# Making the state's part of an SSD output transposed, with a loaded decay row and ScalarE arguments, in a hybrid SSD and attention layer

## The chip, the cores and the metric

The kernel runs on one core of one Trainium2 chip. A core has five engines with an instruction queue each: TensorE (PE; its weight loads are listed apart as PEld), VectorE (DVE), ScalarE (ACT), GpSimd (POOL) and SyncE (SP). The metric is the time of one execution on the device in microseconds (us), the median of several runs. A profiled execution gives the span and the trace.

## What is computed

One decoder layer over 512 tokens and 16 meta tokens in front of them, with model width 1024: a Mamba-2 state space (SSD) branch of 32 heads of 64 columns in 4 groups, a forgetting-attention branch, a gated sum of both, an output projection and a norm. All is float32. The change lies in the SSD branch, whose core in the reference is (cut):

```python
xdt = xh * dt                                  # per chunk of 128 tokens, per head
a_cs = jnp.cumsum(dt * a, axis=-1)             # cumulative log decay
seg = a_cs[..., :, None] - a_cs[..., None, :]
decay = jnp.exp(jnp.where(causal, seg, -jnp.inf))
cb = jnp.einsum("bclgn,bcsgn->bcgls", cm, bm)
y_diag = jnp.einsum("bcgls,bcgrls,bcsgrp->bclgrp", cb, decay, xdt)
states = jnp.einsum("bclgn,bcgrl,bclgrp->bcgrpn", bm, jnp.exp(a_cs[..., -1:] - a_cs), xdt)
# scan over chunks: h_in[c+1] = h_in[c] * exp(a_cs[c, -1]) + states[c]
y_off = jnp.einsum("bclgn,bcgrpn,bcgrl->bclgrp", cm, h_in, jnp.exp(a_cs))
y = y_diag + y_off + d_skip * x
```

The reference is `y_off`: the state h (128 state rows by 8 heads of 64 columns for a group) multiplied by C, each token's row scaled by exp of that head's cumulative decay at that token.

## The kernel before

**Matrix products.** Large products (`gemm`, L106) split both operands into a high and a low part and issue three matmuls for each slice: high by high, low by high, high by low. A weight block arrives in `raw` by a DMA of SyncE; ScalarE makes the high part `whi` (a 128x1024 cast, L90) and VectorE the low part `wlo` (L91). Their results go to one of two PSUM tiles `mm`. All other products go to one of four PSUM tiles `ax`.

**The SSD branch.** It is done group by group, `ssd_gemm(g)` and then `ssd_core(g)`. `ssd_gemm` makes x, B and C of the group (`conv`: the PSUM tile is copied by ScalarE to `xp`, L380, then four taps) and the gate z. `ssd_core` goes over five chunks: c = 0 is the 16 meta tokens, c = 1 to 4 are 128 tokens each. Channels lie on partitions (two heads of 64 in a tile of 128) and tokens along the row in x, z and the result `yd`; h has the state dimension on partitions and the group's 512 columns along the row. For each chunk:

- PE transposes x into `px` (four 128x128, L440). VectorE makes `xdt` (L443) and `xdd` (L446) of it.
- `ab`, a 128x1024 tile from the ring `big4` of four buffers, is filled by a GpSimd DMA (L449, 512 KB, each row of the cumulative decay sent to all 128 partitions). VectorE subtracts the decay of the row's own token and takes the minimum with 0, one head at a time (eight instructions, L451), ScalarE takes exp (L453), VectorE multiplies by the causal C·B product.
- `py` is C times h: the chunk of C is the stationary operand and h, 512 columns, moves (L456). ScalarE copies it to `y`, eight instructions of 64 columns, each with the decay factor `eac` of a head as scale (L460).
- `pst` is the chunk's state (L466). For the next h, GpSimd multiplies h by the chunk decay (L471) and VectorE adds `pst` (L472).
- `pt` collects the result, tokens along the row: four transposes of `y` (L477) and on top of them eight products of `xdt` with `ab`, y_diag (L481). VectorE adds it to `yd` (four instructions, L486).

An `ax` tile of a chunk takes the slot of the tile of the same kind one chunk earlier: `py` of chunk c can start only when `py` of chunk c-1 has been read.

**Around it.** While the chunks of group g run, PE fills the time between their steps with other products: in group 0 the `conv` products of the next group; in the others `s_group(g-1)`, the projection of the group that was finished before. Its 128x512 results are copied by ScalarE in `s_group(0)`, which lies among the chunks of group 1 (`ms`, L691), and added by VectorE in the others (L693). The four buffers of `big4` are shared by the groups, so the DMA of `ab` for chunk c of group g+1 waits on GpSimd's queue until y_diag of chunk c of group g has been made.

**What sets the order.** The code is written group by group, but the order of the instructions on each engine comes from a scheduler of the tile framework, which places them by its own cost model before the kernel is built; sections marked `raised` come first when ready. On the chip each engine runs its list in this fixed order: an instruction that waits holds all behind it on that engine.

## Time and profile before

| what | value |
|---|---|
| median of 3 runs | 852.7 us (852.65 to 852.73) |
| the profiled execution, its own time | 853.14 us |
| its span | 851.4 us |
| PE busy | 834.7 us, 98% |
| DVE busy | 601.8 us, 71% |
| ACT busy | 442.5 us, 52% |
| POOL busy | 72.1 us, 8% |

The span is the time between the first and the last instruction that the trace shows; the profiled execution's time is 1.74 us longer. Busy time is the union of the instructions' own durations on an engine; an engine that waits for data or for a free buffer is idle. The chunks of the four groups lie between about 90 and 405 us.

### The profile page before, as it was taken

How to read it: one execution, taken by the hardware profiler on the slowest of the kernel's cores; microseconds unless marked ns; L12 is line 12 of the kernel's file. 1: busy time of each engine (PE TensorE's matmuls, PEld its weight loads, DVE VectorE, ACT ScalarE, POOL GpSimd, SP SyncE). 2: the span in 40 equal slices, each digit the busy share in tenths (PEclk: the TensorE clock that was granted, in tenths of full speed). 3: DMA queues.
4: the chain of work that ended last, by engine and by line, in shares of the span. 5: the costliest groups of instructions: out<-in, count | busy, mean ns of one | idle time of the engine just before them, and what ended most of it. 6: DMA issues, size and time to landing. Idle time of an engine off the chain costs nothing.

```text
span 851.4 us, 13318 instructions
## 1 busy us (share of the span) xinstructions
PE 834.7 (98%) x5037; PEld 722.9 (85%) x5037; DVE 601.8 (71%) x1296; ACT 442.5 (52%) x906; POOL 72.1 (8%) x136
## 2 busy tenths in 40 slices
PE   6999999999999999999999999999999999999996
PEld 4998889778987799778898988888888898888885
DVE  7799598946994689746786766666767666647735
ACT  6455455445543366333574666566666666522332
POOL 3031110011000100011100001000000100000000
PEclk9999999999999999999999999999999999999999
DMA  7245344235332453222322222222322222224422
GB/s 214 76 127 162 78 110 112 77 96 115 89 96 79 96 123 99 88 62 51 86 91 76 75 75 76 75 76 75 77 75 76 76 75 75 75 84 166 146 75 99
DMA packets 114500, 79.94 MB, mean 94 GB/s; under 512 B 5684, under 2 KB 108260, under 8 KB 114436
## 3 DMA queue, kind: packets, MB, share of 16 engines
q1 hardware_dynamic: 110692, 70.08, 28.9%
q0 software_dynamic: 3744, 9.01, 5.2%
q8 instruction: 39, 0.64, 0.3%
q14 instruction: 25, 0.20, 0.1%
HBM read 76.65 MB, written 2.44 MB: 93 GB/s over the span
## 4 chain that ended last, share of the span: by engine, by line
PE 90%; DMA 3%; DVE 3%; issue 2%; ACT 0%; POOL 0%; SPq 0%; DVEq 0%; POOLq 0%
PE mm L106 71%; PE ax L657 3%; PE mm L781 3%; PE ax L631 2%; DMA big<-acs_d 2%; PE ax L781 1%; PE ax L481 1%; PE ax L596 1%; PE ax L466 1%; PE ax L595 1%; PE ax L456 1%; PE ax L440 1%; DMA big<-in_x_dram 1%; DVE big L451 1%; PE ax L477 1%
## 5 line engine op out<-in xcount | busy, mean ns | idle before, releaser
L106 PE MATMUL mm<-ulo,whi 128*128 128x264 f32 (+1 forms) x1024 | 286.5, 328 | 0.0
L106 PE MATMUL mm<-uhi,whi 128*128 128x264 f32 (+1 forms) x1024 | 284.5, 327 | 0.0
L90 ACT CAST whi<-raw 128x1024 fp32r<-128x1024 f32 x118 | 124.2, 1052 | 143.4 <-PE mm L106 115.4
L91 DVE TENSOR_TENSOR wlo<-raw,whi 128x1024 fp32r<-128x1024 f32 x117 | 142.8, 1220 | 68.4 <-ACT whi L90 31.5
L106 PE MATMUL mm<-uhi,wlo 128*128 128x264 f32 (+1 forms) x1024 | 189.4, 326 | 0.0
L106 PEld LDWEIGHTS mm<-uhi,whi 128*128 128x128 f32 x1024 | 172.3, 188 | 16.9 <-issue 2.7
L106 PEld LDWEIGHTS mm<-ulo,whi 128*128 128x128 f32 x1024 | 172.4, 188 | 16.3 <-issue 2.9
L106 PEld LDWEIGHTS mm<-uhi,wlo 128*128 128x128 f32 x1024 | 152.6, 188 | 14.5 <-issue 0.7
L106 PE MATMUL mm<-yhi,whi 128*128 128x512 f32 x192 | 78.6, 409 | 0.7 <-ACT ms L691 0.7
L106 PE MATMUL mm<-ylo,whi 128*128 128x512 f32 x192 | 76.6, 399 | 0.0
L601 ACT ACTIVATE tmp<-tmp,nmx 128x400 f32<-128x400 f32 (+4 forms) x80 | 41.2, 517 | 28.1 <-DVE nmx L598 26.0
L384 DVE SCALAR_TENSOR_TENSOR xbc<-xp,hcol,xbc 128x528 f32<-128x528 f32 x72 | 54.1, 763 | 0.5 <-ACT tmp L387 0.3
L106 PE MATMUL mm<-yhi,wlo 128*128 128x512 f32 x192 | 54.1, 401 | 0.0
L598 DVE CUSTOM_DVE_ANT_0 tmp<-ax,maskf 128x288 f32<-128x288 f32 (+4 forms) x80 | 32.7, 434 | 23.3 <-PE ax L596 23.0
L451 DVE TENSOR_SCALAR big<-big,dtok 128x128 f32<-128x128 f32 x128 | 28.8, 289 | 27.2 <-DMA big<-acs_d 27.2
L460 ACT ACTIVATE tmp<-ax,eac 128x64 f32<-128x64 f32 x128 | 28.2, 330 | 34.8 <-PE ax L456 34.8
L106 PEld LDWEIGHTS mm<-yhi,whi 128*128 128x128 f32 x192 | 36.1, 188 | 10.7 <-issue 2.3
L106 PEld LDWEIGHTS mm<-ylo,whi 128*128 128x128 f32 x192 | 36.1, 188 | 9.5 <-issue 2.6
L106 PEld LDWEIGHTS mm<-yhi,wlo 128*128 128x128 f32 x192 | 35.8, 188 | 9.2 <-issue 2.2
L657 PE MATMUL ax<-big,vt 128*128 128x512 f32 (+2 forms) x144 | 35.4, 329 | 0.0
L453 ACT ACTIVATE big<-big 128x1024 f32<-128x1024 f32 x16 | 17.0, 1061 | 33.9 <-DVE big L451 33.9
L693 DVE TENSOR_TENSOR ms<-ms,mm 128x512 f32<-128x512 f32 x24 | 16.5, 686 | 23.3 <-PE mm L106 23.3
(258 smaller groups left out, 1167.3 us busy)
## 6 DMA issues: line engine op xcount, KB each, us to landing
raw<-in_w_in_dram SPq DMA_DIRECT2D x88, 512.0 KB, 3.8
big<-acs_d POOLq DMA_DIRECT2D x16, 512.0 KB, 6.2
raw<-in_w_proj_ssd_dram SPq DMA_DIRECT2D x16, 512.0 KB, 3.4
raw<-in_w_proj_att_dram SPq DMA_DIRECT2D x8, 512.0 KB, 3.4
raw<-in_w_out_dram SPq DMA_DIRECT2D x8, 512.0 KB, 3.5
big<-in_x_dram SPq DMA_DIRECT2D x4, 512.0 KB, 6.5
yhi<-in_x_dram SPq DMA_DIRECT2D x2, 1024.0 KB, 6.9
out_dram<-big SPq DMA_DIRECT2D x3, 512.0 KB, 2.6
```

Source lines behind the costliest of these rows:

```text
L90: S.copy(hi, raw)
L91: (GP if nparts[0] <= 1 else V).tensor_sub(lo, raw, hi.bitcast(F32))
L106: PE.matmul(o, lw, u[:, a:b], start=i == 0, stop=i == len(seq) - 1)
L384: V.scalar_tensor_tensor(o, xp[:, k:k + L], cw[:, 24 * k + ct:24 * k + ct + 1], o, op0=ALU.mult, op1=ALU.add)
L451: V.tensor_scalar(ab[:, i], ab[:, i], ac_t[:, c, g * HG + i:g * HG + i + 1], 0.0, op0=ALU.subtract, op1=ALU.min)
L453: S.activation(ab, ab, AF.Exp)
L460: S.activation(y[:, i * 64:(i + 1) * 64], py[:, i * 64:(i + 1) * 64], AF.Copy, scale=eac[:, c, g * HG + i:g * HG + i + 1])
L598: V.tensor_tensor_reduce(pr[i][:, a:b], o, m, -1.0, 3e38, ALU.add, ALU.min, nmx[:, n:n + 1])
L601: S.activation(pr[i][:, a:b], pr[i][:, a:b], AF.Exp, bias=nmx[:, i:i + 1], scale=-1.0, accum_out=rsum[:, n:n + 1])
L631: PE.transpose(dest[b, i], pr[i][:, s0:s0 + P], ident)
L657: PE.matmul(po[:, o:T], w, q, start=i == 0, stop=i == len(seq) - 1)
L781: PE.matmul(pss[s][t], a, b, start=kq == 0 and i == 0, stop=kq == 3 and i == len(seq) - 1)
```

## The change

For chunks 1 to 4 of each group, 16 in all:

- The arguments of the decay matrix are made by ScalarE: eight `Relu` with scale -1 and the row token's decay as bias, in place of the eight VectorE instructions; the exp that follows has scale -1. (relu(a - b) with a minus in front is the minimum of b - a and 0.)
- `py` is made transposed: four products, each with 128 columns of h as stationary operand and the chunk of C (128 columns) moving.
- A tile `eb` (from the ring `tmp`) gets the cumulative decays of the chunk by two GpSimd DMAs, each sending four rows of 128 to 64 partitions; ScalarE takes exp of it (128x512), VectorE multiplies it by `py`.
- `pt` holds y_diag alone. VectorE adds it to `eb`, and the four instructions that add to `yd` read `eb`.
- The eight scaled copies of ScalarE, the four transposes of `y`, and the tile `eac` with its exp are gone.

```diff
--- before.py
+++ after.py
@@ -71,7 +71,7 @@
         return axp.tile([P, 512], F32, tag="ax", name=nm("ax"))
 
     V, S, PE, GP = nc.vector, nc.scalar, nc.tensor, nc.gpsimd
-    HE, UE, SE, YS_ACT = GP, V, V, True
+    HE, UE, SE = GP, V, V
 
     def raised(n=1):
         return tc.high_priority(offset=n * 1000000)
@@ -369,8 +369,6 @@
     V.tensor_mul(dtd, dtd, dt_t)
     dch = cst.tile([P, 5, 32], F32, name="dch")
     S.activation(dch, lastv, AF.Exp)
-    eac = cst.tile([P, 5, 32], F32, name="eac")
-    S.activation(eac, ac_t, AF.Exp)
 
 
     def conv(ps, ct, o):
@@ -448,19 +446,18 @@
                 ab = big4((P, HG, P))
                 nc.gpsimd.dma_start(out=ab, in_=acs_d[hs, a:b].partition_broadcast(P))
                 for i in range(HG):
-                    V.tensor_scalar(ab[:, i], ab[:, i], ac_t[:, c, g * HG + i:g * HG + i + 1], 0.0,
-                                    op0=ALU.subtract, op1=ALU.min)
-                S.activation(ab, ab, AF.Exp)
+                    S.activation(ab[:, i], ab[:, i], AF.Relu, bias=ac_t[:, c, g * HG + i:g * HG + i + 1], scale=-1.0)
+                S.activation(ab, ab, AF.Exp, scale=-1.0)
                 V.tensor_mul(ab, ab, cbt[:, c - 1].unsqueeze(1).broadcast_to([P, HG, P]))
+                eb = row("tmp", (P, T))
+                for e in range(2):
+                    nc.gpsimd.dma_start(out=eb[64 * e:64 * e + 64].rearrange("p (j l) -> p j l", j=4),
+                                        in_=acs_d[g * HG + e:(g + 1) * HG:2, a:b].partition_broadcast(64))
+                S.activation(eb, eb, AF.Exp)
                 py = ax_ps()
-                PE.matmul(py, ct[:, a:b], h, start=True, stop=True)
-                y = row("tmp", (P, T))
-                if YS_ACT:
-                    for i in range(HG):
-                        S.activation(y[:, i * 64:(i + 1) * 64], py[:, i * 64:(i + 1) * 64], AF.Copy,
-                                     scale=eac[:, c, g * HG + i:g * HG + i + 1])
-                else:
-                    V.tensor_mul(heads(y), heads(py), hb(eac[:, c, hs]))
+                for j in range(4):
+                    PE.matmul(py[:, j * P:(j + 1) * P], h[:, j * P:(j + 1) * P], ct[:, a:b], start=True, stop=True)
+                V.tensor_mul(eb, py, eb)
             if c < 4:
                 pst = ax_ps()
                 PE.matmul(pst, btok[0:n, c], xdd[0:n], start=True, stop=True)
@@ -473,19 +470,17 @@
                 h = h2
             if c:
                 pt = ax_ps()
-                for j in range(4):
-                    PE.matmul(pt[:, j * P:(j + 1) * P], y[:, j * P:(j + 1) * P], ident,
-                              is_transpose=True, start=j == 0, stop=False)
                 for i in range(HG):
                     r = (i % 2) * 64
                     PE.matmul(pt[r:r + 64, (i // 2) * P:(i // 2 + 1) * P],
-                              xdt[:, i * 64:(i + 1) * 64], ab[:, i], start=False,
+                              xdt[:, i * 64:(i + 1) * 64], ab[:, i], start=i < 2,
                               stop=i >= HG - 2)
                 o = (c - 1) * P
+                V.tensor_add(eb, pt, eb)
                 for j in range(4):
                     V.scalar_tensor_tensor(
                         yd[j][:, o:o + P], yd[j][:, o:o + P], dcol[:, 4 * g + j:4 * g + j + 1],
-                        pt[:, j * P:(j + 1) * P], op0=ALU.mult, op1=ALU.add)
+                        eb[:, j * P:(j + 1) * P], op0=ALU.mult, op1=ALU.add)
         sm = row("tmp", (P, T))
         for j in range(4):
             UE.tensor_mul(yd[j], yd[j], zs[j])
```

The scheduler orders the changed program anew. Below are rows of the lists before and after at three places, in group 1. A row is a source line, the operation, output and inputs with buffer numbers, shape and count. The changed file's lines are lower by a few: its L438 (px transposes) was L440, L449 (Relu) takes the place of L451, L450 (exp) was L453, L459 (py) was L456, L463 (state) was L466, L475 (y_diag) was L481, L468 (h multiplied) was L471, L447 (DMA of `ab`) was L449, L686 (copy to `ms`) was L691; L454 (two DMAs of `eb`) and L456 (its exp) are new.

PE before, from the transposes of `y` of chunk 2 to the product of C and h of chunk 3:

```order
L106 MATMUL mm_2144<-yhi_1227,wlo_2140 128x512 x4
L477 MATMUL ax_1838<-ident,tmp_1824 128x128
L440 MATMUL ax_1855<-ident,xbc_1373 128x128
L440 MATMUL ax_1855<-ident,xbc_1439 128x128
L440 MATMUL ax_1855<-ident,xbc_1505 128x128
L440 MATMUL ax_1855<-ident,xbc_1571 128x128
L477 MATMUL ax_1838<-ident,tmp_1824 128x128 x3
L481 MATMUL ax_1838<-big_255_1810,tmp_1806 64x128 x8
L456 MATMUL ax_1876<-h_1835,xbc_1242 128x512
```

PE after, from the product of h and C of chunk 2 to the transposes of x for chunk 3:

```order
L459 MATMUL ax_1858<-xbc_1224,h_1816 128x128 x4
L106 MATMUL mm_2074<-yhi_1209,wlo_2070 128x512 x3
L463 MATMUL ax_1864<-tmp_1840,vt_1767 128x512
L475 MATMUL ax_1869<-big_264_1842,tmp_1838 64x128 x8
L438 MATMUL ax_1883<-ident,xbc_1355 128x128
L438 MATMUL ax_1883<-ident,xbc_1421 128x128
L438 MATMUL ax_1883<-ident,xbc_1487 128x128
L438 MATMUL ax_1883<-ident,xbc_1553 128x128
```

The transposes L477, which lay among those of x ahead of y_diag, are gone; the product with h is four instructions, and y_diag stands directly behind the state product.

ACT before, from chunk 2 to chunk 4 of group 1 (`big_399` and `big_408` are `ab` tiles of group 2, `ax_1876` and `ax_1930` are `py`):

```order
L460 ACTIVATE tmp_1824<-ax_1822,eac 128x64 x8
L691 COPY ms_2136<-mm_2123 128x512
L691 COPY ms_2157<-mm_2144 128x512
L460 ACTIVATE tmp_1878<-ax_1876,eac 128x64 x8
L90 CAST whi_2213<-raw_2212 128x1024
L691 COPY ms_2172<-mm_2159 128x512
L453 ACTIVATE big_399_2779<-big_399_2779 128x1024
L691 COPY ms_2193<-mm_2180 128x512
L460 ACTIVATE tmp_1932<-ax_1930,eac 128x64 x8
L90 CAST whi_2278<-raw_2277 128x1024
L691 COPY ms_2208<-mm_2195 128x512
```

ACT after, the same stretch (`tmp_1854` and `tmp_1904` are `eb` of chunks 2 and 3 of group 1, `dtok` holds the biases):

```order
L686 COPY ms_2066<-mm_2053 128x512
L449 ACTIVATE big_399_2745<-big_399_2745,dtok 128x128 x8
L686 COPY ms_2087<-mm_2074 128x512
L456 ACTIVATE tmp_1854<-tmp_1854 128x512
L450 ACTIVATE big_399_2745<-big_399_2745 128x1024
L90 CAST whi_2141<-raw_2140 128x1024
L686 COPY ms_2102<-mm_2089 128x512
L449 ACTIVATE big_408_2795<-big_408_2795,dtok 128x128 x8
L456 ACTIVATE tmp_1904<-tmp_1904 128x512
L450 ACTIVATE big_408_2795<-big_408_2795 128x1024
L686 COPY ms_2123<-mm_2110 128x512
```

The scaled copies of `py` are gone; the Relus of the next group's `ab` stand ahead of the exp of `eb`, of the 128x1024 exp and of copies to `ms`.

POOL before, in group 1 (`h_1835` to `h_1943` are the states, `big_399` and the following are `ab` of group 2):

```order
L471 TENSOR_TENSOR h_1835<-h_1799,dch 128x512
L471 TENSOR_TENSOR h_1889<-h_1835,dch 128x512
L449 DMA big_399_2779<-acs_d 128x8x128
L471 TENSOR_TENSOR h_1943<-h_1889,dch 128x512
L449 DMA big_408_2833<-acs_d 128x8x128
L449 DMA big_417_2887<-acs_d 128x8x128
L449 DMA big_425_2939<-acs_d 128x8x128
```

POOL after:

```order
L454 DMA tmp_1804<-acs_d 64x4x128 x2
L468 TENSOR_TENSOR h_1816<-h_1781,dch 128x512
L468 TENSOR_TENSOR h_1866<-h_1816,dch 128x512
L447 DMA big_399_2745<-acs_d 128x8x128
L454 DMA tmp_1854<-acs_d 64x4x128 x2
L468 TENSOR_TENSOR h_1916<-h_1866,dch 128x512
L447 DMA big_408_2795<-acs_d 128x8x128
L454 DMA tmp_1904<-acs_d 64x4x128 x2
L447 DMA big_417_2845<-acs_d 128x8x128
L454 DMA tmp_1952<-acs_d 64x4x128 x2
```

Two DMAs of `eb` for each chunk have come in; those of chunks 2 to 4 stand behind the DMA of `ab` of the next group, which waits for y_diag of the chunk before.

## Rows read from the trace of the kernel before

**Rows 1.** The page: the span, then busy time of the engines

```profile
span 851.4 us, 13318 instructions
PE 834.7 (98%) x5037; PEld 722.9 (85%) x5037; DVE 601.8 (71%) x1296; ACT 442.5 (52%) x906; POOL 72.1 (8%) x136
```

**Rows 2.** Busy time in stretches: length, PE, PEld, DVE, ACT, POOL, clock

```profile
...
62.00:130.00 68.00, 67.16 (x461) 57.52 (x460) 57.16 (x129) 36.74 (x74) 10.06 (x17) 1.00 0.50 125
...
160.00:210.00 50.00, 48.61 (x296) 37.98 (x295) 29.79 (x66) 22.41 (x53) 6.68 (x7) 1.00 0.38 89
...
```

**Rows 3.** Waits of PE from 90 to 405 us: total, times, longest

```profile
PE ax L456 <- DVE h L472: 1.8, 3, 0.7
PE mm L106 <- ACT ms L691: 0.7, 1, 0.7
PE ax L466 <- DVE tmp L446: 0.3, 1, 0.3
```

**Rows 4.** Timeline of PE, last chunks of group 3: start, length, instruction

```profile
...
388.45 0.60 PE L440 MATMUL ax<-ident,xbc 128*128 128x128 f32 x4
388.88 0.49 PE L477 MATMUL ax<-ident,tmp 128*128 128x128 f32 x3
389.31 1.09 PE L481 MATMUL ax<-big,tmp 128*64 128x128 f32 x16
390.33 0.50 PE L106 MATMUL mm<-yhi,whi 128*128 128x512 f32 x1
390.67 0.39 PE L106 MATMUL mm<-ylo,whi 128*128 128x512 f32 x1
390.90 0.39 PE L106 MATMUL mm<-yhi,whi 128*128 128x512 f32 x1
...
392.06 1.02 PE L456 MATMUL ax<-h,xbc 128*128 128x512 f32 x2
392.52 0.79 PE L106 MATMUL mm<-ylo,whi 128*128 128x512 f32 x1
393.15 0.63 PE L106 MATMUL mm<-yhi,wlo 128*128 128x512 f32 x2
```

**Rows 5.** Timeline of PE at group 0: four 128x128 products, and what follows

```profile
71.44 1.05 PE L421 MATMUL ax<-xbc,xbc 128*128 128x128 f32 x8
72.33 0.60 PE L424 MATMUL ax<-ident,xbc 128*128 128x128 f32 x4
```

**Rows 6.** Groups by shape: busy us, mean ns of one, idle before

```profile
...
L90 ACT CAST whi<-raw 128x1024 fp32r<-128x1024 f32 x118 | 124.2, 1052 | 143.4 <-PE mm L106 115.4 <-issue 11.9 <-PE mm L781 6.3
...
L451 DVE TENSOR_SCALAR big<-big,dtok 128x128 f32<-128x128 f32 x128 | 28.8, 289 | 27.2 <-DMA big<-acs_d 27.2
...
L460 ACT ACTIVATE tmp<-ax,eac 128x64 f32<-128x64 f32 x128 | 28.2, 330 | 34.8 <-PE ax L456 34.8
...
L387 ACT ACTIVATE tmp<-xbc 128x528 f32<-128x528 f32 x24 | 14.0, 634 | 2.2 <-DVE xbc L384 2.0
...
L443 DVE TENSOR_TENSOR tmp<-ax,dtok 128x512 f32<-128x512 f32 x16 | 11.0, 687 | 5.9 <-PE ax L440 5.9
...
L691 ACT COPY ms<-mm 128x512 f32<-128x512 f32 x8 | 4.8, 596 | 7.6 <-PE mm L106 7.6
...
```

**Rows 7.** Timeline of GpSimd in group 1

```profile
190.17 1.03 POOL L471 TENSOR_TENSOR h<-h,dch 128x512 f32<-128x512 f32 x1 [8.02 <-DVE h L472]
191.16 0.92 POOL L449 DMA_DIRECT2D big<-acs_d  x1
```

**Rows 8.** Timeline of VectorE in the same stretch

```profile
196.63 1.66 DVE L451 TENSOR_SCALAR big<-big,dtok 128x128 f32<-128x128 f32 x8 [4.32 <-DMA big<-acs_d]
```

**Rows 9.** Timeline of ScalarE in the same stretch

```profile
192.41 1.75 ACT L460 ACTIVATE tmp<-ax,eac 128x64 f32<-128x64 f32 x8 [1.36 <-PE ax L456]
```

**Rows 10.** Line L449, the transfers of cumulative decays

```profile
DMA to landing us min/median/max: 5.3/6.2/9.8
```

**Rows 11.** Issues of transfers: size, median us from issue to landing

```profile
z<-qr_d POOLq DMA_DIRECT2D x16, 8.0 KB, 2.2
```

## Prediction

> **What bounds the kernel now.** The page comes first: PE is busy 834.7 of 851.4 us [rows 1]. Busy time by stretch comes next, because a mean over the span hides where the idle time lies. The stretches shown ran at a granted clock of 1.00, the upper of TensorE's two levels (2.4 GHz), and PE was idle 68.00 - 67.16 = 0.84 us in one and 50.00 - 48.61 = 1.39 us in the other [rows 2]. The list of waits says on what: in the 315 us that hold all chunks, PE waited 1.8 + 0.7 + 0.3 = 2.8 us, most of it for the state h ahead of the product with C [rows 3]. So PE is the bound, and the edits count in two ways only: by PE time that they take out, and by waits of PE that they end or make. ScalarE and VectorE are not full, but each works in a fixed order, and what stands behind a waiting instruction can hold PE.
>
> **PE's work.** Four transposes of x take 388.88 - 388.45 = 0.43 us; the last three of `y`, with the turn to y_diag behind them, take 0.43 too [rows 4]. The turn stays, since y_diag then follows the state product, so I take the price of the clean four: 64 transposes of `y` go, 64 x 0.43 / 4 = -6.9 us (by the three it would be -9.2). Between 392.06 and 393.15 lie the old product with h and one L106 matmul, which takes 390.90 - 390.67 = 0.23: the old product takes 1.09 - 0.23 = 0.86 us [rows 4]. Four 128x128 products, the new form, take 72.33 - 71.44 = 0.89 us (each leaves two records) [rows 5]. That is 16 x 0.03 = +0.5. Net **-6.4 us**. Nothing else on PE changes in number.
>
> **VectorE.** Out go eight instructions per chunk, 1.66 us [rows 8]; in come a multiply and an add of 128x512, 0.69 each by the like row L443 [rows 6]: -0.3 us per chunk. The four adds to `yd` read SBUF where they read PSUM; no row shows that form of them, so I keep their price; if they took half or twice the time (only the norm of the group waits for them), PE would not see it. VectorE also waited 27.2 us for the `ab` transfers [rows 6]; that wait moves to ScalarE with the Relus. By itself this is worth nothing, since PE is the bound.
>
> **ScalarE.** Out go eight copies of 64 columns: 1.75 us [rows 9], 330 ns of one, so starts lie (1.75 - 0.33) / 7 = 0.20 apart. The width price, from the 528-column activation (634 ns) to the 1024-column cast (1052 ns), is 418 / 496 = 0.84 ns a column [rows 6], so a Relu of 128 columns is 330 + 54 = 384 ns, and eight take 7 x 0.26 + 0.38 = 2.2 us. Bounds: 1.75 (as the copies) and 8 x 0.384 = 3.1 (no overlap); each end would change the sum below by 0.45 or 0.9 at four places, -1.8 or +3.6. I take 2.2, because the overlap of the copies is a row. The exp of `eb` adds 0.63 (L387 is its size). Per chunk 2.2 + 0.63 - 1.75 = +1.1 us, 17 us in all. ScalarE is busy 22.41 of 50.00 us in group 1's stretch [rows 2], so as a sum this hides. As an order it doesn't, see the walk.
>
> **GpSimd.** Two more DMA issues per chunk. The 512 KB issue takes 0.92 [rows 7]; for 128 KB I take between half of that and the whole, 1.0 to 1.8 us for two, hidden as long as the multiply of h behind them is early. Landing of `eb`: no row has this shape; the nearest are 2.2 us (8 KB) [rows 11] and 5.3 to 9.8 us (512 KB to 128 partitions, median 6.2) [rows 10]. I take 5, nearer to the larger since its rows repeat as often: `eb` is issued about 1 us behind `ab`, lands 0.5 us after it, and ScalarE comes to it 2.8 us after `ab` has landed (eight Relus and a copy). So it costs nothing up to a landing of about 7 us, and above that holds the exp one for one.
>
> **The waits that go.** The 1.8 us for h came where the product with h stood soon behind the add of the state. In the new PE list, 9 to 12 L106 matmuls (2 to 2.7 us) stand between y_diag and that product, and the add takes 0.7. I count all 2.8 us as gone, and price the new waits in full.
>
> **The waits that come.** The `ab` transfer of the next group is issued when y_diag of this chunk is done and GpSimd's multiply of h is behind it (1.03 us, then the issue [rows 7]). It landed 196.63 - 191.16 = 5.47 us after its issue [rows 7, 8]. Before, VectorE waited there. Now ScalarE does, ahead of eight Relus; and behind them on ScalarE stand the exp of `eb`, without which VectorE can't read `py` and the next `py` has no buffer, and in group 1 the copies to `ms`, without which the L106 products have no buffer.
>
> The walk of group 1 in the new order, zero at the first state product. PE prices: state or `py` 0.9, y_diag 390.33 - 389.31 = 1.0, four transposes 0.43, L106 0.23 [rows 4]. `py` of chunk 1 ends at 4.9, eight L106 and the state product at 7.6, y_diag of chunk 1 at 8.6. VectorE's add of h ends at 8.4, GpSimd's multiply at 9.5, then `ab` is issued and lands at 15.0. Relus to 17.2, a copy to `ms` (0.6, [rows 6]) to 17.8, exp of `eb` to 18.4, VectorE's multiply to 19.2: now the buffer is free. PE comes to `py` of chunk 3 at 18.6: it waits about 0.7. For chunk 3 the chain is: y_diag ends 23.4, `ab` lands 28.9, Relus 31.1, a cast `whi` 32.2 (1.05), exp of `eb` 32.8, the 128x1024 exp 33.9, copy to `ms` 34.5; PE wants that `mm` tile at 32.6 and waits about 1.9. Group 1: **+2.6 us**. The same walk of group 0, with 264-column L106 at 264/512 of 0.23, gives `py` of chunk 3 a wait of 1.3 and of chunk 4 one of 0.8: **+2.1 us**. In group 2 the copies to `ms` are VectorE's, ScalarE reaches `eb` 0.6 earlier and PE comes 0.2 later: nothing. Group 3 has no next group: nothing. Together +4.7.
>
> **The sum.** The profiled span 851.4 - 6.4 - 2.8 + 4.7 = 846.9, that is -4.5. The profiled execution took 853.14, the median is 852.7; the difference goes to the median: 848.2.
>
> **A rule against the change.** ScalarE does the arguments in 2.2 us where VectorE took 1.66 [rows 6, 8, 9]. The Trainium skill, page "ScalarE: Activation LUTs", section "Rules for kernel authors", says that relu, max, min, add and mul belong on VectorE and not on ScalarE; no run here shows a Relu yet. By the same page's section "What ACT_TABLE_LOAD costs" (280 ns + 0.833 ns a column, some 93 ns overlap) my estimate for eight is about 2.4 us, which would put 0.2 us more on each waiting chain, +0.8 in the sum. What the rule would do here is the last rival below.
>
> **Rivals.**
> - No new waits. A chain shorter by 0.7 to 1.9 us in all four places ends them. For it: the Relus at their lower bound give 0.45, and the cast in the longest chain (1.05) may stand clear of it. Against it: the landing of 5.47 can hardly shrink, its least is 5.3 [rows 10]. Then -6.4 - 2.8 = -9.2: 843.5 us.
> - The gain is given back. Landings at their median, 6.2 [rows 10], are 0.7 later than in the walk: up to +2.8 at the four places, PE's waits 7.5. An `eb` that lands after 8 us holds its exp 1 us more, at three or four of them: 10.9. The time is then 851.0 to 854.4. For it: the four orders have no slack left. Against it: a wait in chunk 3 also moves what chunk 4 needs, so that not all add up.
> - ScalarE becomes the gate: slower. The Relus hold ScalarE's queue until a late `ab` has landed, and the exp of `eb`, the copies to `ms` and the casts stand behind. It decides from 6.4 + 2.8 = 9.2 us of new waits on, 9.2 / 12 = 0.77 for each of the twelve next-group transfers. With landings of 6.8, between median and most, 1.3 later than in the walk, the four places wait 4.7 + 5.2 = 9.9, and the four transfers of group 2, where the walk leaves a few tenths of slack, 0.5 each: 11.9, or +2.7: 855.4 us. For it: landings of up to 9.8 [rows 10]. Against it: VectorE has waited 27.2 us for the same transfers [rows 6], and PE's waits for VectorE's h come to 1.8 only [rows 3].
> - The change doesn't do what it says (transposes not gone): excluded by the PE list.
>
> **How the numbers follow.** Within 0.2% (1.7 us: 851.0 to 854.4) is about what a measurement can't tell from no change. Forecast, 844.5 to 851.0: 0.50. No new waits, near 843.5: 0.12. Given back: 0.20. Slower than 854.4: 0.18. Faster 0.62, same 0.20, slower 0.18. The range 843.4 to 855.0 takes in the second and the third case and leaves most of the last outside; the forecast's own range is 844.5 (Relus at the lower bound and one of the waits less) to 851.0.
>
> **What would show it.** PE instructions L477 gone and PE's busy time lower by 6 to 7 us; eight Relus at 2.2 us; PE waits at `py` (L459) on VectorE's multiply (L460) in groups 0 and 1, 0.7 to 1.3 each; one L106 wait on a copy to `ms` in group 1 of about 2; ScalarE idle for `big<-acs_d` in place of VectorE. Wrong if PE waits more than 7 us there, if `eb` lands later than the Relus end, if group 2 waits too, or if the order of the attention part, placed anew, costs or gives anything after 410 us.

## The result

The changed kernel takes 847.62 us (median of 4 runs, 847.39 to 848.29) where the kernel before takes 852.67 in the same set (4 runs, 852.28 to 852.73): a ratio of 0.9937, 95% interval 0.9925 to 0.9948, or -5.1 us. The forecast was 848.2. The profiled execution took 847.58 us with a span of 845.9, so the span is 5.5 us shorter than in [rows 1].

The page of the changed kernel, span and busy time, answers to [rows 1]:

```profile
span 845.9 us, 13372 instructions
PE 826.0 (98%) x5069; PEld 720.2 (85%) x5069; DVE 599.0 (71%) x1200; ACT 458.8 (54%) x921; POOL 89.6 (11%) x168
```

PE lost 8.7 us of busy time and ScalarE gained 16.3 (17 had been worked out). Of the 8.7, 1.8 are no work saved: in the first 20 us the transposes of L250 show as 8.2 us busy and 0.1 idle in the kernel before, as 6.2 busy and 1.9 idle in the changed one, and PE starts the line behind them at 17.26 and 17.06 us, nearly the same. That leaves 6.9 where 6.4 was worked out. The PE count is higher although 64 transposes are gone, since each new product leaves eight records and the old one left two.

Busy time by stretch, with the columns of [rows 2]:

```profile
62.00:130.00 68.00, 68.00 (x490) 59.88 (x489) 53.32 (x85) 52.37 (x114) 14.77 (x25) 1.00 0.61 145
160.00:210.00 50.00, 46.91 (x315) 39.29 (x315) 31.40 (x62) 29.51 (x61) 10.50 (x14) 1.00 0.58 128
```

In the first stretch PE's idle 0.84 us is gone. In the stretch of group 1 its idle time has grown from 1.39 to 50.00 - 46.91 = 3.09 us, at a granted clock of 1.00 (2.4 GHz) as before.

The waits of PE from 80 to 405 us, which answer to [rows 3]:

```profile
PE mm L106 <- ACT ms L686: 3.1, 1, 3.1
PE ax L495 <- DVE tmp L492: 0.6, 1, 0.6
PE ax L463 <- DVE tmp L444: 0.5, 1, 0.5
```

The 1.8 us for h are gone. The wait on a copy to `ms` has grown from 0.7 to 3.1 us, the state product's wait for `xdd` is 0.5 where it was 0.3, and 0.6 is new, in the norm of a group. Together PE waits 4.2 us where it waited 2.8.

The chain that ended last, over that wait (start, length, what was done or waited for; "issue" is time without a wait that the profile shows):

```profile
...
180.50 0.86 PE ax L463 x2
181.36 1.05 PE ax L475 x16
182.41 0.28 issue
182.69 6.99 DMA big<-acs_d
...
190.30 1.85 ACT big L449 x6
192.15 0.93 ACT whi L90
193.09 0.53 ACT tmp L456
193.62 0.95 ACT big L450
194.56 0.48 ACT ms L686
...
195.09 11.54 PE mm L106 x83
...
```

This is that wait in order of time. PE ends y_diag of chunk 3 at 182.41. GpSimd then issues the next group's `ab`, which takes 6.99 us to land. ScalarE is idle for the last 2.91 us of it, because the eight Relus come next in its list; then a cast, the exp of `eb`, the exp of `ab`, and only then the copy to `ms` at 194.56 that frees the `mm` tile. PE had run out of other work 3.09 us before it starts again at 195.09.

Groups of instructions by shape, for what the change brought (busy us, mean ns of one, idle before it), and the timeline row of the eight Relus in that chain:

```profile
...
L449 ACT ACTIVATE big<-big,dtok 128x128 f32<-128x128 f32 x128 | 39.6, 389 | 32.8 <-DMA big<-acs_d 32.8
...
L454 POOL DMA_DIRECT2D tmp<-acs_d x32 | 20.0, 629 | 1.8 <-issue 1.2 <-DVE xbc L386 0.7
...
L456 ACT ACTIVATE tmp<-tmp 128x512 f32<-128x512 f32 x16 | 10.0, 626 | 9.8 <-DMA tmp<-acs_d 9.8
...
```

```profile
...
189.70 2.45 ACT L449 ACTIVATE big<-big,dtok 128x128 f32<-128x128 f32 x8 [2.91 <-DMA big<-acs_d]
...
```

Landings of `ab` (line L447 in the changed file), which answer to [rows 10]:

```profile
DMA to landing us min/median/max: 5.2/6.7/8.8
```

The median landing is 6.7 us where it was 6.2.

### The profile page after: what moved, and what is told of

The parts are those of the page before. It is cut to its first block, busy times and chain, and to the rows that moved or that the text cites. A ratio compares the mean times of both kernels' runs of the same rounds, so it can differ in the third digit from the quotient of the medians.

```text
span 845.9 us, 13372 instructions
## 1 busy us (share of the span) xinstructions
PE 826.0 (98%) x5069; PEld 720.2 (85%) x5069; DVE 599.0 (71%) x1200; ACT 458.8 (54%) x921; POOL 89.6 (11%) x168
## 3 DMA queue, kind: packets, MB, share of 16 engines
HBM read 80.84 MB, written 2.44 MB: 98 GB/s over the span
## 4 chain that ended last, share of the span: by engine, by line
PE 91%; DVE 3%; DMA 3%; ACT 2%; issue 0%; SPq 0%; DVEq 0%; ACTq 0%
PE mm L106 71%; PE ax L652 3%; PE mm L776 3%; PE ax L626 2%; DMA big<-acs_d 2%; PE ax L463 2%; PE ax L475 2%; PE ax L776 1%; PE ax L459 1%; PE ax L591 1%; PE ax L590 1%; PE ax L438 1%; DMA big<-in_x_dram 1%; DVE big L808 1%; ACT big L449 1%
## 5 line engine op out<-in xcount | busy, mean ns | idle before, releaser
L106 PE MATMUL mm<-uhi,whi 128*128 128x264 f32 (+1 forms) x1024 | 283.0, 326 | 0.0
L106 PE MATMUL mm<-ulo,whi 128*128 128x264 f32 (+1 forms) x1024 | 281.7, 325 | 0.0
L106 PE MATMUL mm<-uhi,wlo 128*128 128x264 f32 (+1 forms) x1024 | 187.9, 325 | 0.0
L106 PEld LDWEIGHTS mm<-uhi,whi 128*128 128x128 f32 x1024 | 171.9, 188 | 15.0 <-DVE z L410 0.3
L106 PEld LDWEIGHTS mm<-ulo,whi 128*128 128x128 f32 x1024 | 172.0, 188 | 13.4
L106 PEld LDWEIGHTS mm<-uhi,wlo 128*128 128x128 f32 x1024 | 151.6, 188 | 13.8 <-issue 0.5
L106 PE MATMUL mm<-yhi,whi 128*128 128x512 f32 x192 | 76.4, 398 | 3.1 <-ACT ms L686 3.1
L106 PE MATMUL mm<-ylo,whi 128*128 128x512 f32 x192 | 75.4, 393 | 0.0
L449 ACT ACTIVATE big<-big,dtok 128x128 f32<-128x128 f32 x128 | 39.6, 389 | 32.8 <-DMA big<-acs_d 32.8
L106 PE MATMUL mm<-yhi,wlo 128*128 128x512 f32 x192 | 54.4, 397 | 0.0
L593 DVE CUSTOM_DVE_ANT_0 tmp<-ax,maskf 128x144 f32<-128x144 f32 (+4 forms) x80 | 33.0, 434 | 17.4 <-PE ax L591 17.0
L106 PEld LDWEIGHTS mm<-yhi,whi 128*128 128x128 f32 x192 | 36.1, 188 | 10.5 <-ACT ms L686 3.5
L106 PEld LDWEIGHTS mm<-ylo,whi 128*128 128x128 f32 x192 | 36.1, 188 | 6.8
L106 PEld LDWEIGHTS mm<-yhi,wlo 128*128 128x128 f32 x192 | 35.3, 188 | 7.1 <-issue 0.5
L637 DVE TENSOR_TENSOR big<-ax,big 128x512 fp32r<-128x512 f32 (+1 forms) x48 | 27.7, 598 | 5.4 <-ACT big L636 5.3
L460 DVE TENSOR_TENSOR tmp<-ax,tmp 128x512 f32<-128x512 f32 x16 | 11.0, 690 | 24.2 <-ACT tmp L456 16.7
L652 PEld LDWEIGHTS ax<-big,vt 128*128 128x128 f32 x144 | 24.2, 188 | 2.8
```

The lines of the kernel that those rows point to most:

```text
L106: PE.matmul(o, lw, u[:, a:b], start=i == 0, stop=i == len(seq) - 1)
L449: S.activation(ab[:, i], ab[:, i], AF.Relu, bias=ac_t[:, c, g * HG + i:g * HG + i + 1], scale=-1.0)
L593: V.tensor_tensor_reduce(pr[i][:, a:b], o, m, -1.0, 3e38, ALU.add, ALU.min, nmx[:, n:n + 1])
L637: V.tensor_sub(l, src, h.bitcast(F32))
L652: PE.matmul(po[:, o:T], w, q, start=i == 0, stop=i == len(seq) - 1)
```

## The experiments

After the result, the theory was: the gain is PE's work (64 transposes out, -6.4 us net), plus the 2.8 us of waits of before, less the 4.2 us of now, of which 3.1 hang on the transfer of `ab` in front of the Relus. That makes -5.0, and -5.1 was measured. The first rival was that VectorE's relief is the gain: it no longer waits 27.2 us for transfers [rows 6], so h is on time. The others stand with the runs. Each set of runs has its own times of the kernel before (medians 852.67 to 853.94 us), and the ratios are against those; where a version is set against the changed kernel, the difference of the medians is given first and then that of the ratios, times 853 us.

### One half of the change at a time

The arguments back on VectorE, the rest of the change kept:

```diff
-                    S.activation(ab[:, i], ab[:, i], AF.Relu, bias=ac_t[:, c, g * HG + i:g * HG + i + 1], scale=-1.0)
-                S.activation(ab, ab, AF.Exp, scale=-1.0)
+                    V.tensor_scalar(ab[:, i], ab[:, i], ac_t[:, c, g * HG + i:g * HG + i + 1], 0.0,
+                                    op0=ALU.subtract, op1=ALU.min)
+                S.activation(ab, ab, AF.Exp)
```

> The transposed product with the loaded decay row stays; the arguments go back to VectorE (subtract and minimum, eight instructions), and the exp that follows has scale 1 again. Theory (PE's work is the gain): the 64 transposes stay out, -6.4 us against the kernel before; ScalarE is no longer held by the transfers, so PE's one wait of 3.1 us for a copy to ms, seen in the changed kernel, is gone; VectorE is held by them as before, at most 2.8 us of PE waits. Time 844.5 to 848. Rival (the gain is VectorE's relief: it no longer waits 27.2 us for transfers): most of the gain is lost, 850 to 853.

Measured: 848.13 us (6 runs, 846.87 to 852.65), ratio 0.9952 (0.9934 to 0.9970). The median lies 0.13 us past the theory's upper end and outside the rival's 850 to 853, but the interval reaches up to 850.7, and two of the six runs lie in the rival's range. Those two ran at a mean granted clock of 0.990 and 0.991; the other four, 846.87 to 848.14 us, at 0.996 to 0.998 (see the last section). PE's waits, in the profiled execution, the longest of the six:

```profile
PE mm L106 <- DVE z L410: 1.1, 1, 1.1
PE ax L496 <- DVE tmp L493: 1.0, 1, 1.0
PE mm L106 <- DVE ylo L514: 0.7, 1, 0.7
PE ax L460 <- DVE h L470: 0.6, 1, 0.6
```

The wait for `ms` is down to 0.2 us, and others came, most of them on VectorE's gate, norm and split instructions; the wait for h (L460 on L470) is 0.6 us, although VectorE makes the arguments again. So the place of the product in the new list does most of what ended that wait in the changed kernel.

The other half alone, the kernel before with the Relus and nothing else:

```diff
-                    V.tensor_scalar(ab[:, i], ab[:, i], ac_t[:, c, g * HG + i:g * HG + i + 1], 0.0,
-                                    op0=ALU.subtract, op1=ALU.min)
-                S.activation(ab, ab, AF.Exp)
+                    S.activation(ab[:, i], ab[:, i], AF.Relu, bias=ac_t[:, c, g * HG + i:g * HG + i + 1], scale=-1.0)
+                S.activation(ab, ab, AF.Exp, scale=-1.0)
```

> The kernel before with the arguments made by ScalarE (Relu) and nothing else: the product with h, its eight scaled copies and the transposes of y stay. Theory: no PE work is removed; ScalarE holds the transfers' wait and behind it the scaled copies, the copies to ms and the casts, so PE waits at least the 2.8 us of before and more: 853 to 858. Rival (VectorE's relief is the gain): 847 to 850.

Measured: 849.44 us (5 runs), ratio 0.9956 (0.9944 to 0.9968): -3.8 us. The theory's 853 to 858 is missed on the wrong side, and the rival's range holds the time. PE's only wait in 80 to 405 us:

```profile
PE mm L106 <- ACT xp L380: 0.5, 1, 0.5
```

All 2.8 us of [rows 3] are gone, with the transposes and the scaled copies still there, and with the product with h as close behind y_diag as before. VectorE's relief is therefore a gain of its own. That leaves -3.8 + 2.3 = -1.5 us that PE's waits don't show; 0.5 of it lies ahead of the first chunk in the profiled executions, where PE comes to L364 at 61.13 us here and at 61.66 in the kernel before.

The two halves do not add up. The Relus alone took off 3.8 us, but on top of the transposed product they bring nothing that these runs show: without them it takes 846.87 to 848.14 us at the higher clock, with them 847.39 to 848.29.

### The transposes

Taken out of the kernel before, so that the state's part is missing from the output:

```diff
-                for j in range(4):
-                    PE.matmul(pt[:, j * P:(j + 1) * P], y[:, j * P:(j + 1) * P], ident,
-                              is_transpose=True, start=j == 0, stop=False)
...
-                              xdt[:, i * 64:(i + 1) * 64], ab[:, i], start=False,
+                              xdt[:, i * 64:(i + 1) * 64], ab[:, i], start=i < 2,
```

> The kernel before with the four transposes of y per chunk left out, so the state's part is missing from the output; the product with h and the eight scaled copies still run. Theory: 64 transposes at 0.108 us are worth 6.9 us of PE, and PE waits less since y_diag needs no copy: 843 to 846. Rival (transposes lie beside other work or in PE's waits, so that taking them out brings little): 849 to 852.

Measured: 842.62 us, ratio 0.9879 (0.9865 to 0.9894): -10.3 us by the ratio, somewhat more than either expected. PE's waits fell to one of 0.4 us:

```profile
PE ax L456 <- DVE h L472: 0.4, 1, 0.4
```

Of the 10.3, 6.9 are the row price and 2.8 - 0.4 = 2.4 the waits. 1.0 stays; 0.4 of it lies ahead of the first chunk (L364 at 61.29 us).

The opposite, 64 transposes added to the changed kernel, those of x made twice:

```diff
-            for j in range(4):
+            for j in list(range(4)) * (2 if c else 1):
                 PE.transpose(px[0:n, j * P:(j + 1) * P], xs[j][:, a:b], ident)
```

> The changed kernel with the four transposes of x of each full chunk made twice into the same tile: 64 more transposes on PE, nothing else. It prices a transpose in place. By the row price of 0.108 us: +6.9 us, 854.5. Leaving out 64 transposes of y gave -10.5 us; if that was all the price of transposes (0.164 us each), +10.5: 858. If part of PE's time is hidden in waits for other engines, less than +6: under 853.5.

Measured: 854.55 us (11 runs, 853.26 to 857.53), ratio 1.0022 (1.0014 to 1.0031): 854.55 - 847.62 = 6.9 us above the changed kernel, or 7.3 by the ratios. That the median meets the row price to a tenth is in part chance. PE's waits from 80 to 405 us are 2.5 us here instead of 4.2, and some runs lost time to a lower clock: the profiled one, 857.53 us, up to 5 us (granted clock 0.72 from 12 to 24 us and 0.57 from 204 to 208). The run with the highest mean clock, 0.999, took 853.26, which is 5.6 us above the changed kernel; with the 1.7 us of waits that went, 7.3. So the price from the timeline, 0.43 us for four, holds in place within some tenths for all 64. What leaving out transposes gave beyond it is not their price.

### The wait for the copy to ms

The copies made by VectorE:

```diff
                 if g == 0:
                     msd[d] = st("ms", [P, T], 8)
-                    S.copy(msd[d], ps)
+                    V.tensor_copy(msd[d], ps)
```

> The changed kernel with the copies to ms of the first projection (group 1's stretch) made by VectorE instead of ScalarE. Theory: PE's wait of 3.1 us is the copy standing behind the Relus on ScalarE; it goes, and PE's list of waits between 80 and 400 us has no such entry: 844.3 to 845.0. Rival (the stretch is full, and another wait takes its place, VectorE's multiply that waits for the exp of the loaded row holding the copy): 847 to 848.

Measured: 844.59 us (4 runs, 844.36 to 844.95), ratio 0.9900 (0.9887 to 0.9913): 3.0 us below the changed kernel (3.2 by the ratios). PE's waits:

```profile
PE mm L106 <- DVE ms L686: 1.6, 1, 1.6
PE ax L463 <- DVE tmp L444: 0.2, 1, 0.2
```

Half of the wait has moved to VectorE, so the theory's list of waits was wrong there. The copy, at 194.84 us, stands behind a low part `wlo` that waited for ScalarE's cast `whi`, which ScalarE makes behind the Relus:

```profile
192.38 1.22 DVE L91 TENSOR_TENSOR wlo<-raw,whi 128x1024 fp32r<-128x1024 f32 x1 [3.03 <-ACT whi L90]
```

The time is as the theory had it, since of the two smaller waits one went and the other shrank to 0.2. This version beats both kernels.

The control, the same edit in the kernel before:

> The kernel before with nothing but the copies to ms of the first projection made by VectorE. It is the control of the run in which the same edit took 3 us off the changed kernel. Theory (that edit is worth what PE waits for ms: 3.1 us in the changed kernel, 0.7 in the one before, where VectorE also carries the wait for the transfers of ab): 852 to 854, no gain. Rival (the edit is worth 3 us in any kernel of this form, so it says nothing of the change): 849 to 850.5.

Measured: 855.46 us (7 runs, 854.74 to 857.59), ratio 1.0029 (1.0018 to 1.0040): slower than its set's 853.94 by 1.5 us, or 2.5 by the ratio, more than expected. The profiled execution, 854.97 us, lost 4 x 0.43 = 1.7 us to a lower clock (last section). PE waits now for `xdd` (L466 on L446), since VectorE has the copies and the transfers both:

```profile
PE ax L466 <- DVE tmp L446: 3.4, 2, 3.1
PE ax L456 <- DVE h L472: 0.4, 1, 0.4
```

So the 3 us belong to the changed kernel's ScalarE list, not to the edit.

### What makes the transfer late

The loads of the decay row left out, the exp reading another tile, so that the decay factors are missing:

```diff
-                for e in range(2):
-                    nc.gpsimd.dma_start(out=eb[64 * e:64 * e + 64].rearrange("p (j l) -> p j l", j=4),
-                                        in_=acs_d[g * HG + e:(g + 1) * HG:2, a:b].partition_broadcast(64))
-                S.activation(eb, eb, AF.Exp)
+                S.activation(eb, cbt.rearrange("p c l -> p (c l)"), AF.Exp)
```

> The changed kernel without the two loads of the decay row per chunk: its exp reads another tile of the same size that is there already, so the decay factors are missing from the output. Theory A (the new loads make the transfers of ab land later, 6.7 us median and 7.0 us for the one on which the copy to ms hangs, against 5.5 before): the landing falls by 0.5 to 1.5 us, PE's wait of 3.1 us falls to 1.5 to 2.5, 845.5 to 847. Theory B (landings vary by themselves, and the loads and their GpSimd time are hidden): 847.3 to 848.

Measured: 843.75 us, ratio 0.9896 (0.9883 to 0.9909), 3.9 us below the changed kernel (3.5 by the ratios) and beyond theory A's range on its side. PE's waits and the landings of `ab`:

```profile
PE ax L492 <- DVE tmp L489: 0.4, 1, 0.4
PE mm L106 <- ACT xp L378: 0.3, 1, 0.3
```

```profile
DMA to landing us min/median/max: 5.3/5.7/8.8
```

The median landing is 5.7 us instead of 6.7 and the wait for `ms` is gone. The prediction had costed the loads at nothing. But the run does not show that the landing is the whole cause. The order was made anew: in ScalarE's list the sixth of the eight copies to `ms`, the one that held PE in the changed kernel, now stands ahead of the Relus that wait for the transfer issued at 185.19 us:

```profile
189.16 0.58 ACT L683 COPY ms<-mm 128x512 f32<-128x512 f32 x1
190.49 2.46 ACT L449 ACTIVATE big<-big,dtok 128x128 f32<-128x128 f32 x8 [0.75 <-DMA big<-acs_d]
```

Nor do the landings always differ as these two medians do: in the seven profiles with the row loads on GpSimd's queue the medians of `ab` are 6.2 to 6.7 us, in the seven without loads there 5.7 to 6.2.

The loads on SyncE's queue:

```diff
-                    nc.gpsimd.dma_start(out=eb[64 * e:64 * e + 64].rearrange("p (j l) -> p j l", j=4),
+                    nc.sync.dma_start(out=eb[64 * e:64 * e + 64].rearrange("p (j l) -> p j l", j=4),
```

> The changed kernel with the two loads of the decay row issued by SyncE's queue, where the weights are issued, instead of GpSimd's. Theory (the loads on GpSimd's queue, 1.24 us of issues and their landing, hold ab, the exp and through ScalarE the copy to ms): as with the loads left out, most of the 3.1 us goes: 844 to 845.5, and ScalarE's 9.8 us of waiting for the row falls under 3. Rival A (any traffic beside ab makes it late, whatever queue): 846.5 to 848. Rival B (a row load that waits for its buffer on SyncE's queue holds weight loads behind it): PE waits for whi, 848 or more.

Measured: 846.41 us (6 runs, 844.74 to 848.56), ratio 0.9924 (0.9909 to 0.9940). The median falls between the theory and rival A, so the run is inconclusive on the time. The three runs of 844.74 to 845.70 us had a mean granted clock of 0.997 to 0.998, the three of 847.12 to 848.56 one of 0.993 to 0.997, so a part of the spread can be the clock. The issues show a part of the effect (size, median us to landing):

```profile
big<-acs_d POOLq DMA_DIRECT2D x16, 512.0 KB, 5.8
tmp<-acs_d SPq DMA_DIRECT2D x32, 128.0 KB, 4.1
```

The median landing of `ab` is 5.8 us and PE's wait for `ms` is 1.6 us. The transfer on which that copy hangs still took 6.45 us (issued at 183.40, its Relus start at 189.85); the copy also comes earlier because it now stands ahead of the 128x1024 exp. And ScalarE waited 20.3 us for the row instead of 9.8, where under 3 was expected, because its exp moved to an earlier place in the list.

Both edits, SyncE's queue and the copies on VectorE:

> The loads of the decay row on SyncE's queue and the copies to ms on VectorE, on top of the changed kernel. Theory: both end the same wait of PE, so the floor is PE's work: 843 to 844. If the two work on different waits: under 843. Rival B of the run before (weights held): 846 or more.

Measured: 844.75 us, ratio 0.9904 (0.9891 to 0.9917). It misses the expected floor by 0.75 us, and over the copies alone it brings nothing: both edits work on the same wait, which is 1.6 us with either alone and 1.3 with both.

Five buffers for `ab` and eight for `tmp`:

```diff
-BUFS = {"tmp": 10, "xbc": 13, "z": 4, "xp": 2, "h": 2, "big4": 4, "raw": 3, "whi": 2, "wlo": 2, "y": 2, "vt": 2, "mcol": 3}
+BUFS = {"tmp": 8, "xbc": 13, "z": 4, "xp": 2, "h": 2, "big4": 5, "raw": 3, "whi": 2, "wlo": 2, "y": 2, "vt": 2, "mcol": 3}
```

> The changed kernel with five buffers for ab in place of four (and eight for tmp in place of ten, to make room), so each transfer of ab is issued one chunk earlier, some 7 us. Theory (PE's wait hangs on ScalarE waiting for a transfer ahead of the Relus): ScalarE waits for big<-acs_d under 5 us in place of 32.8, PE's wait of 3.1 us is gone: 844 to 845.3. Rival (ScalarE's own work, not the transfer, makes the copy late): 847 or more.

Measured: 848.14 us (6 runs, 844.74 to 849.20), ratio 0.9940 (0.9927 to 0.9953): no gain over the changed kernel in the median, as the rival had it. But the run did not separate the two. ScalarE still waits for the transfers, 32.6 us from 90 to 405 where the changed kernel has 32.8:

```profile
ACT big L449 <- DMA big<-acs_d: 32.6, 9, 10.0
```

The scheduler used the fifth buffer to move the Relus up with the transfers: GpSimd issues five of them in a row at the start (55.91 us) where the changed kernel issues four, and in the stretch of group 1 the first Relus start at 174.74 us as they did at 174.84, now on the tile of the next chunk. The wait was moved, not shortened. The time is not the rival's either: PE's wait for `ms` fell to 2.3 us, and right behind it the granted clock was 0.57 from 194 to 198 us. Eight L106 matmuls took 3.46 us there (194.33 to 197.79) where they took 1.94 in the changed kernel (195.09 to 197.03), so this cost 1.5 us. The one run with a mean clock of 0.999 took 844.74 us, the other five, at 0.995 to 0.998, 847.64 to 849.20.

Five buffers and the copies on VectorE:

> Five buffers for ab (eight for tmp) and the copies to ms on VectorE, on top of the changed kernel. Theory: the two edits end the same wait, so together they bring little over one of them: PE's waits between 80 and 400 us under 1 us, 843 to 844.5. Rival (eight tmp buffers cost): 845 or more.

Measured: 844.78 us, ratio 0.9906 (0.9893 to 0.9919), again the time of the copies alone, within a few tenths; the theory's upper end was 844.5.

### A buffer of its own for the product with h

```diff
-    axp = pool("axp", 4, space=PSUM)
+    axp = pool("axp", 3, space=PSUM)
+    pyp = pool("pyp", 1, space=PSUM)
...
-                py = ax_ps()
+                py = pyp.tile([P, 512], F32, tag="py", name=nm("py"))
```

> The changed kernel with a PSUM buffer of its own, one, for the product with h, and three for the other ax tiles, so that the product of a chunk can start only when VectorE's multiply of the chunk before has read it: the wait that the prediction put at 0.7 to 1.3 us at three places and that the changed kernel did not show. Theory (it did not show because the product takes the buffer of another tile that is free): now it shows, as waits of L460 or as a later place of the product in PE's list: 849 to 852. Rival (the multiply is early enough anyway): 847 to 848.5.

Measured: 854.09 us (12 runs, 852.75 to 856.50), ratio 1.0016 (1.0006 to 1.0027), above both ranges, so the time does not tell the theory from the rival. PE waits for VectorE's multiply once, for 0.5 us, and in group 0 the product of chunk 3 has moved behind the state product and into y_diag. Most of the loss lies elsewhere, in the last stretches:

```profile
720.00:800.00 80.00, 77.23 (x364) 63.86 (x363) 55.75 (x112) 35.08 (x71) 1.05 (x2) 0.98 0.29 99
800.00:854.00 54.00, 45.36 (x191) 36.07 (x189) 24.03 (x48) 14.86 (x29) 0.00 (x0) 0.94 0.26 98
```

PE is idle there for 2.77 and 8.64 us. Of the 8.64, about 7.1 are the end of every kernel here, behind PE's last product (before: 51.40 us from 800 on, 44.29 busy). New are two waits:

```profile
PE mm L107 <- ACT yhi L669: 2.8, 1, 2.8
PE mm L777 <- DVE fpr L796: 2.2, 1, 2.2
```

Behind both the granted clock was 0.72 (778 to 784 and 826 to 832 us), up to 12 x 0.28 = 3.4 us more. The last product of the kernel takes four `ax` tiles, and there are three now; that this makes the two waits is likely, but was not tested.

Why the changed kernel showed no wait for `py` can be read from its own trace. At the three places of the prediction (chunks 3 and 4 of group 0, chunk 3 of group 1) the product with h started before VectorE's multiply of the chunk before:

```profile
102.11 1.05 PE L459 MATMUL ax<-xbc,h 128*128 128x128 f32 x8
103.46 0.69 DVE L460 TENSOR_TENSOR tmp<-ax,tmp 128x512 f32<-128x512 f32 x1 [2.02 <-ACT tmp L456]
...
107.77 1.05 PE L459 MATMUL ax<-xbc,h 128*128 128x128 f32 x8
111.51 0.69 DVE L460 TENSOR_TENSOR tmp<-ax,tmp 128x512 f32<-128x512 f32 x1 [3.70 <-ACT tmp L456]
...
178.05 1.05 PE L459 MATMUL ax<-xbc,h 128*128 128x128 f32 x8
178.33 0.69 DVE L460 TENSOR_TENSOR tmp<-ax,tmp 128x512 f32<-128x512 f32 x1 [1.54 <-ACT tmp L456]
```

PE wrote the new `py` 1.35, 3.74 and 0.28 us before VectorE began to read the old one, so the two lay in different buffers, as the theory had it.

## Why the prediction was right, and where it was not

**PE's work, -6.4.** Right. The price of a transpose held in place (6.9 to 7.3 us for 64), and the chain shows the new product at 0.89 us, as taken. PE's busy time behind the first 20 us fell by 6.9.

**The waits that go, 2.8.** Nearly right: the 1.8 us for h are gone, the 0.3 at the state product stayed, as 0.5. The reason given for h, the product's place behind 9 to 12 L106 matmuls, is half of it. With the arguments on VectorE it leaves 0.6 us; with the arguments on ScalarE and the old place, none. Either is nearly enough.

**The waits that come, 4.7.** The sum was near (4.2) by luck, and the parts were wrong. This is the step that failed. Three of the four waits, 0.7 + 1.3 + 0.8 = 2.8 us, were put on `py` waiting until VectorE had read the `py` of the chunk before. The changed kernel shows none on line L459: at all three places the product started before that read. The rule behind them, that an `ax` tile takes the slot of its own kind one chunk earlier, does not hold there. The fourth, on the copy to `ms`, was mis-sized: 1.9 predicted, 3.1 measured. The place, the order of events and y_diag's end (23.4 us after the first state product by the walk; in the trace that starts at 158.79, so 182.41 - 158.79 = 23.6) were right; `ab` took 6.99 us to land instead of 5.47, which is +1.5, and the Relus 2.45 instead of 2.2. The 1.2 us more on `ms`, the 0.6 in the norm and the 0.5 at the state product, none of them in the sum, made up for most of the 2.8 that did not come.

**The Relus' price.** 389 ns and 2.45 us for eight, where 384 and 2.2 were taken; the overlap of the shorter copies did not carry over. The Trainium skill, page "ScalarE: Activation LUTs", section "What ACT_TABLE_LOAD costs", gives 280 + 0.833 x 128 = 387 ns and an overlap of 93, by which my estimate for eight is 7 x 294 + 387 = 2.44 us: the trace agrees, with 2.45. Its section "Rules for kernel authors", which puts relu on VectorE, did not decide here. Relus alone took 3.8 us off, and 1.8 of it were waits for VectorE's h, which its list held and not its speed.

**GpSimd and the row load, nothing.** Wrong: leaving the loads out took 3.5 to 3.9 us off, and the wait of 3.1 us for `ms` with it. The issues (0.63 us of one) were within the bounds. The landing (median 5.6 us, most 8.1) passed the 7 us up to which it was to cost nothing; ScalarE waited 9.8 us for it, all in group 3, and no wait of PE came of that. What was left out is that the loads are not alone: with them on GpSimd's queue the transfers of `ab` landed later, about 0.6 us in the mean of the medians, and with and without them the scheduler places the copies to `ms` differently. How much of the 3.1 us is the one and how much the other was not separated.

**What stays open.** The Relus alone gave 1.5 us, and taking out the transposes 1.0 us, more than PE's listed waits and the row prices account for; 0.5 and 0.4 of this came ahead of the first chunk, and the rest has no cause here. Whether the row load delays `ab` through GpSimd's queue or through traffic is not settled: on SyncE's queue the median landing recovered, but the exp moved too.

## What to carry to other kernels

When work that waits for a transfer moves to another in-order engine, list what stands behind it there and who waits for that; the wait moves with the work, and its new price is paid by the queue behind it. A scheduled list doesn't keep the places of its tiles or instructions: read which buffer a tile got, and after adding a buffer look whether the wait moved along. A small load has to be priced by what it does to the large transfer beside it and to the order around it, and not by its own landing alone. Where a kernel's runs spread over 3 us, look at their granted clock before reading a difference of medians.

## What the runs showed of the hardware

In the kernel with the arguments on VectorE, the granted clock fell after a pause of PE. Busy time by stretch of its profiled execution, with the columns of [rows 2]:

```profile
150.00:155.00 5.00, 5.00 (x25) 4.14 (x24) 4.97 (x8) 3.86 (x7) 0.00 (x0) 1.00 0.35 105
155.00:160.00 5.00, 3.42 (x24) 2.54 (x22) 5.00 (x8) 3.63 (x8) 0.00 (x0) 1.00 0.00 0
160.00:165.00 5.00, 4.31 (x10) 2.57 (x11) 5.00 (x8) 0.00 (x0) 0.00 (x0) 0.71 0.38 105
165.00:170.00 5.00, 5.00 (x15) 3.23 (x14) 4.27 (x5) 0.59 (x1) 3.06 (x3) 0.61 0.00 0
170.00:175.00 5.00, 5.00 (x39) 3.76 (x38) 2.58 (x4) 2.63 (x4) 0.80 (x2) 1.00 0.47 91
```

PE was idle 1.58 us from 155 to 160 and 0.69 in the next 5 us, and the granted clock went from 1.00 (2.4 GHz) to 0.71 and 0.61, between the two levels of 2.4 and 1.2 GHz, and back. At those values the ten microseconds lost 5 x 0.29 + 5 x 0.39 = 3.4 us of PE at full clock. With two more such stretches, 12 to 16 us at 0.59 and 314 to 320 at 0.72, this execution lost some 6.7 us. The six runs of that kernel follow it: with a mean clock of 0.990 and 0.991 they took 852.65 and 850.79 us, with 0.996 to 0.998 846.87 to 848.14. The same is seen behind the waits of PE of 2.30 us with five buffers and of 3.06 us with the copies on VectorE in the kernel before:

```profile
194.00:198.00 4.00, 3.67 (x9) 2.93 (x10) 3.93 (x10) 3.12 (x11) 0.00 (x0) 0.57 0.48 132
...
168.00:172.00 4.00, 4.00 (x13) 3.14 (x12) 1.29 (x2) 0.77 (x2) 1.04 (x1) 0.57 0.23 70
```

In these two executions the wait cost its own length and some 1.5 to 1.7 us more in the clock behind it. In the changed kernel PE paused 3.09 us at once and the clock of that stretch stayed at 1.00, so a pause alone doesn't tell. In the profiled executions of nine of the fourteen kernels, those before and after the change among them, no stretch of 2 us ahead of PE's last matmul shows a granted clock under 0.97.
